# Moving the lo subtraction of two weight pieces per round from VectorE to GpSimd in a float32 decoder trunk

## The chip, the cores and the metric

The kernel runs on one NeuronCore of a Trainium2 chip. The metric is the time of one execution on the device in microseconds (us), as the runtime measures it for the core. A few runs of each kernel are timed and the median is quoted; one more execution is taken with the hardware profiler, and its rows are what is read below.

## What is computed

Two decoder layers on 256 tokens of width 2048, in float32. Each layer mixes tokens (differential attention in the first, dilated attention in the second), attends to 256 memory tokens, and ends in an MLP. The change lies in the MLP alone:

```
hm = _rmsnorm(x, g_mlp[i])
x = x + jnp.square(jax.nn.relu(hm @ w_mlp1[i])) @ w_mlp2[i]
```

with `w_mlp1` 2048 x 8192 and `w_mlp2` 8192 x 2048.

## The kernel before

**Precision.** TensorE multiplies in the format fp32r, which keeps fewer bits than float32. So every operand is held as a pair: `hi` is the value rounded to fp32r, made by ScalarE, and `lo` is value minus `hi`. A product is three passes, hi by hi, hi by lo and lo by hi (`passes`, L609 to L612, one matmul each: L610, L611, L612).

**Units and rounds.** The 8192 hidden columns are cut into eight units of 1024. Unit 0 is computed plainly; units 1 to 7 with a scheme of seven block products per step, eight steps (`step_up`) per unit. While a unit is being made, the unit before it is multiplied with `w_mlp2`. One such round c has eight groups g; group g runs one step of a later unit (on PSUM tiles `p1` to `p7`) and then one `group_down` (24 matmuls into `psd`) for a block n = g // 2 of 512 output columns and a token half t = g % 2. For each n the round needs four weight pieces k = 0, 2, 4, 6, sixteen per round, each a tile of 128 x 1024 which serves the matmuls k and k + 1 of `group_down`.

**A piece.** `piece_hi` (L693) loads the piece into `raw_d` by a DMA that SyncE (SP) issues, and ScalarE (ACT) makes `hi_d` (L699). `piece_lo` (L702) makes `lo_d` by a subtraction on VectorE (DVE, L705). The buffer of `raw_d` comes free for a later load when `lo_d` has been made. The pieces with k = 6 use the ring of buffers "ux", which also holds `b` and `o`, the weights of the steps.

**The weights of a step.** `up_weights` (L210) loads `b` and `o` and makes sums and pairs from them: `s` (DVE, L229), `bh` (ACT) and `bl` (DVE), `o` (L233 and L235), `oh`, `sh` and `sl`, `th` and `tl`. On DVE all of these read two tiles in SBUF.

**The passage.** The square of the ReLU of a unit is finished as four blocks `u`. `to_hT` turns them: TensorE transposes a block (four transposes, L688) into the PSUM tile `pu`, ACT writes the hi part of `hT` (L117), DVE the lo part (L118, one input in PSUM and one in SBUF). The four blocks are turned one at a time, two of them inside the step of group 0 and two inside that of group 1, and a PSUM bank is needed for each. This is the passage from one unit to the next: group 0 of rounds 1 to 6, so six in a layer and twelve in the program. At a passage the pieces of n = 0 are made as follows: k = 0 and the hi of k = 2 at the end of the round before, the lo of k = 2 at the start of group 0, k = 4 and k = 6 after its step.

**What sets the order.** This part runs under `tc.manual_schedule()`: every engine executes its instructions in the order in which the code issues them, and semaphores make one engine wait for another. GpSimd (POOL) issues only the DMAs of `add_down` here (L725), which add a finished `part` (made by ACT at L724 from `psd`) to `x_sb`.

Of the kernel before, what the change touches and what calls it, by code (L numbers as in the profile page):

```python
# [9 lines left out]
F32 = mybir.dt.float32  # L10
# [4 lines left out]
ALU = mybir.AluOpType  # L15
# [43 lines left out]
def trunk(ctx: ExitStack, tc: tile.TileContext, x, mem, g_attn, w_in, w_out, lambda_qk,  # L59
          subln_g, g_mem, w_mem_kv, g_mlp, w_mlp1, w_mlp2, g_final, out):  # L60
    nc = tc.nc
# [17 lines left out]
    def load_weights(src, k, c, nm, other=False):  # L79

        if other:
            raw = upool.tile([P, 1024], F32, tag="ux", bufs=UX, name=f"raw_{nm}")
        else:
            raw = wpool.tile([P, 1024], F32, tag="raw", bufs=RAW, name=f"raw_{nm}")
        nc.sync.dma_start(raw.rearrange("p (k c) -> p k c", c=c), src.rearrange("(k p) c -> p k c", p=P))
        return raw
# [355 lines left out]
    for i in range(DEPTH):  # L442
# [194 lines left out]
        def prep_up(c, kp):  # L637

            making = up_weights(w_mlp1[i], kp, c * 1024, f"{i}{c}{kp}")
            for _ in range(3):  # L640
                next(making)
                yield
            facts[c, kp] = next(making)

        def step_up(c, kp, between=None):


            if kp == 0:
                banks[c] = {n: bank([P, 512], f"{n}_{i}{c}", n in ("p1", "p2", "p5", "p7")) for n in facts[c, 0]}
            order = ("p1", "p2", "p6", "p3", "p7", "p5", "p4") if kp == 0 else ("p1", "p3", "p2", "p5", "p7", "p6", "p4")  # L650
            made = facts.pop((c, kp))
            for j, n in enumerate(order):
                if between and j in between:
                    between[j]()
                hi, lo = made[n]
                passes(banks[c][n], comb[kp][:, FACTORS.index(n)], hi, lo, kp == 0, kp == KP - 1)

        def end_up(c):


            nm, ps = f"{i}{c}", banks.pop(c)
            c1, u2, u3, u4 = (work.tile([P, 512], F32, tag="tmp", bufs=TMP, name=f"t{n}_{nm}") for n in range(4))
            nc.scalar.activation(c1, ps["p1"], AF.Copy)
            yield
            c11, m12, c21, m22 = (work.tile([P, 512], F32, tag="ev", bufs=EV, name=f"u{n}_{nm}") for n in range(4))
            nc.vector.tensor_tensor(c11, c1, ps["p2"], op=ALU.add)
            nc.vector.tensor_tensor(u2, c1, ps["p6"], op=ALU.subtract)
            squared(c11, c11, 1.0)
            nc.vector.tensor_tensor(u4, u2, ps["p5"], op=ALU.add)
            nc.vector.tensor_tensor(m12, u4, ps["p3"], op=ALU.add)  # L670
            squared(m12, m12, -1.0)
            nc.vector.tensor_tensor(u3, u2, ps["p7"], op=ALU.add)
            nc.vector.tensor_tensor(m22, u3, ps["p5"], op=ALU.add)
            nc.vector.tensor_tensor(c21, u3, ps["p4"], op=ALU.add)
            ublk[c] = ((c11, 0, 0), (m12, 0, 1), (c21, 1, 0), (m22, 1, 1))
            yield
            squared(c21, c21, 1.0)
            yield
            squared(m22, m22, -1.0)

        def to_hT(c):

            for f in range(2):
                hT[c, f] = act_tile(f"hT{i}{c}{f}")
            for n, (u, t, f) in enumerate(ublk[c]):
                pt = bank([P, 4, P], f"pu_{i}{c}{n}")
                for k in range(4):
                    nc.tensor.transpose(pt[:, k], u[:, k * P:(k + 1) * P], ident)  # L688
                cols = slice(t * P, (t + 1) * P)
                split(hT[c, f][:, :, 0, cols], hT[c, f][:, :, 1, cols], pt)  # L690
                yield

        def piece_hi(c, n, k):  # L693

            r0 = c * 1024 + k * P
            w, nm = w_mlp2[i][r0:r0 + 256, n * 512:(n + 1) * 512], f"d{i}{c}{n}{k}"
            raw = load_weights(w, 2, 512, nm, k == 6)
            hi = wpool.tile([P, 1024], F32R, tag="whi", bufs=WH, name=f"hi_{nm}")
            nc.scalar.activation(hi, raw, AF.Copy)  # L699
            dw[c, n, k] = raw, hi, nm  # L700

        def piece_lo(c, n, k):  # L702
            raw, hi, nm = dw[c, n, k]
            lo = wpool.tile([P, 1024], F32R, tag="wlo", bufs=WH, name=f"lo_{nm}")
            nc.vector.tensor_tensor(lo, raw, hi.bitcast(F32), op=ALU.subtract)  # L705
            dw[c, n, k], dw[c, n, k + 1] = ((hi[:, a:a + 512], lo[:, a:a + 512]) for a in (0, 512))

        def prep_down(c, n, halves):

            for h in halves:  # L710
                for k in (4 * h, 4 * h + 2):
                    piece_hi(c, n, k)
                    piece_lo(c, n, k)
# [37 lines left out]
        def run(steps):  # L751
            for _ in steps:
                pass
# [3 lines left out]
        with tc.manual_schedule():  # L757
            run(prep_up(1, 0))
            prep_down(0, 0, (0,))
            run(first)  # L760
            turned = to_hT(0)
            prep = prep_up(1, 1)
            step_up(1, 0, {2: lambda: (next(turned), next(prep)), 5: lambda: next(turned)})
            run(prep)
            for c in range(NC - 1):
                for g in range(8):
                    uc, kp = (c + 1, g + 1) if g < 7 else (c + 2, 0)
                    pc, pk = (c + 1, g + 2) if g < 6 else (c + 2, g - 6)
                    prep = prep_up(pc, pk) if pc < NC else iter(())
                    n, t = g // 2, g % 2  # L770
                    more = (c, n + 1) if n < 3 else (c + 1, 0)
                    if g == 0 and c:
                        def turn_first():
                            next(turned)
                            next(ending)
                            next(prep)

                        def turn_second():
                            next(turned)
                            next(prep)  # L780

                        turned = to_hT(c)
                        piece_lo(c, 0, 2)
                        step_up(uc, kp, {2: turn_first, 4: turn_second})
                        prep_down(c, 0, (1,))
                        next(prep)
                        run(ending)
                        run(prep)
                    elif g == 0:
                        step_up(uc, kp)  # L790
                        prep_down(c, 0, (1,))
                        run(prep)
                    elif g == 1:
                        step_up(uc, kp, {2: lambda: (next(turned), next(prep)), 4: lambda: run(turned)})
                        run(prep)
                    elif g == 6:
                        step_up(uc, kp)
                        ending = end_up(c + 1)
                        next(ending)
                        run(prep)  # L800
                        next(ending)
                    elif g == 7 and uc < NC:
                        step_up(uc, kp)
                        run(prep)
                        piece_hi(*more, 0)
                        piece_lo(*more, 0)
                    elif g == 7:
                        run(ending)
                        turned = to_hT(c + 1)
                        next(turned)  # L810
                        next(turned)
                        piece_hi(*more, 0)
                        piece_lo(*more, 0)
                    else:
                        step_up(uc, kp)
                        run(prep)
                    if t == 1 and g < 7:
                        prep_down(*more, (0,))
                        piece_hi(*more, 4)
                    add_down(c, n, t, group_down(c, n, t, False))  # L820
                    if t == 1 and g < 7:
                        piece_hi(*more, 6)
                        piece_lo(*more, 4)
                        piece_lo(*more, 6)
                    elif t == 1:
                        piece_hi(*more, 2)
            run(turned)
            piece_lo(NC - 1, 0, 2)
            prep_down(NC - 1, 0, (1,))
# [71 lines left out]
```

## Time and profile before

| | |
|---|---|
| time, median of 3 runs | 2197.18 us (2194.75 to 2198.06) |
| the profiled execution | 2197.42 us |
| its span, first to last instruction | 2195.6 us |
| TensorE (PE) matmul busy | 2169.9 us, 99% |
| VectorE (DVE) busy | 1711.9 us, 78% |
| ScalarE (ACT) busy | 1327.4 us, 60% |
| GpSimd (POOL) busy | 114.0 us, 5% |
| mean granted TensorE clock | 0.998 of full speed |

How to read it: the profiled execution lies 1.8 us above its span and 0.24 us above the median, so sums made against it hold for the median as well. PEld is the weight load of TensorE, which runs beside its matmuls. Rows of a timeline give start and duration in us from the span's start, and in square brackets how long the engine stood idle before the row and what released it; rows of one form that follow each other are merged into one with a count.

### The profile page before, as it was taken

How to read it: one execution, taken by the hardware profiler on the slowest of the kernel's cores; microseconds unless marked ns; L12 is line 12 of the kernel's file. 1: busy time of each engine (PE TensorE's matmuls, PEld its weight loads, DVE VectorE, ACT ScalarE, POOL GpSimd, SP SyncE). 2: the span in 40 equal slices, each digit the busy share in tenths (PEclk: the TensorE clock that was granted, in tenths of full speed). 3: DMA queues.
4: the chain of work that ended last, by engine and by line, in shares of the span. 5: the costliest groups of instructions: out<-in, count | busy, mean ns of one | idle time of the engine just before them, and what ended most of it. 6: DMA issues, size and time to landing. Idle time of an engine off the chain costs nothing.

```text
span 2195.6 us, 28498 instructions
## 1 busy us (share of the span) xinstructions
PE 2169.9 (99%) x10358; PEld 1791.5 (82%) x10358; DVE 1711.9 (78%) x2084; ACT 1327.4 (60%) x1840; POOL 114.0 (5%) x146
## 2 busy tenths in 40 slices
PE   9999999999999999999999999999999999999998
PEld 7888878887888887888888888888788888888886
DVE  6557766667999998999966655566899999999985
ACT  7445555565667666676655544455566666766764
POOL 0000000000000000000000000000000000000000
PEclk9999999999999999999999999999999999999999
DMA  7655555566787877877656555556777778778674
GB/s 235 199 184 163 164 163 181 167 185 216 224 243 199 238 225 209 248 210 219 200 172 192 155 177 178 182 178 185 236 212 233 219 219 235 205 229 239 200 213 149
DMA packets 262399, 443.50 MB, mean 202 GB/s; under 512 B 14497, under 2 KB 80242, under 8 KB 262002
## 3 DMA queue, kind: packets, MB, share of 16 engines
q1 hardware_dynamic: 245856, 412.14, 60.0%
q0 software_dynamic: 16128, 29.37, 7.5%
q8 instruction: 81, 1.33, 0.2%
q14 instruction: 60, 0.49, 0.1%
q10 hardware_dynamic: 274, 0.17, 0.0%
HBM read 409.12 MB, written 3.15 MB: 188 GB/s over the span
## 4 chain that ended last, share of the span: by engine, by line
PE 94%; ACT 2%; DVE 2%; issue 1%; DMA 1%; SPq 0%; POOL 0%; POOLq 0%; DVEq 0%; ACTq 0%
PE psd L611 10%; PE psd L612 10%; PE psd L610 10%; PE p L610 8%; PE p L611 7%; PE p L612 7%; PE ps_k L145 4%; PE ps_q L145 4%; PE pso L166 3%; PE pso L167 3%; PE pso L165 3%; PE ps_q L141 2%; PE ps_k L141 2%; PE psv L165 2%; PE psv L166 2%; PE psv L167 2%
## 5 line engine op out<-in xcount | busy, mean ns | idle before, releaser
L611 PE MATMUL psd<-lo_d,hT 128*128 128x512 f32 x1008 | 392.0, 390 | 0.6 <-DVE lo_d L705 0.6
L612 PE MATMUL psd<-hi_d,hT 128*128 128x512 f32 x1008 | 391.8, 389 | 0.0
L610 PE MATMUL psd<-hi_d,hT 128*128 128x512 f32 x1008 | 391.0, 390 | 0.0
L705 DVE TENSOR_TENSOR lo_d<-raw_d,hi_d 128x1024 fp32r<-128x1024 f32 x252 | 297.4, 1219 | 47.8 <-ACT hi_d L699 47.5
L699 ACT ACTIVATE hi_d<-raw_d 128x1024 fp32r<-128x1024 f32 x252 | 260.2, 1052 | 35.1 <-PE psd L612 13.9
L117 ACT ACTIVATE th<-o 128x1024 fp32r<-128x1024 f32 x112 | 119.0, 1063 | 183.6 <-DVE o L235 157.4
L611 PEld LDWEIGHTS psd<-lo_d,hT 128*128 128x128 f32 x1008 | 189.2, 188 | 40.5 <-DVE lo_d L705 1.5
L612 PEld LDWEIGHTS psd<-hi_d,hT 128*128 128x128 f32 x1008 | 189.2, 188 | 39.9 <-DVE hT L118 0.8
L610 PEld LDWEIGHTS psd<-hi_d,hT 128*128 128x128 f32 x1008 | 189.2, 188 | 39.3
L118 DVE TENSOR_TENSOR bl<-b,bh 128x1024 fp32r<-128x1024 f32 x112 | 136.8, 1221 | 39.0 <-ACT bh L117 39.0
L725 POOL DMA_DIRECT2D x_sb<-part x112 | 96.6, 863 | 1182.1 <-ACT part L724 1176.6
L117 ACT ACTIVATE sh<-s 128x1024 fp32r<-128x1024 f32 x112 | 118.5, 1058 | 54.3 <-DVE s L229 41.7
L118 DVE TENSOR_TENSOR tl<-o,th 128x1024 fp32r<-128x1024 f32 x112 | 137.2, 1225 | 6.2 <-ACT th L117 0.3
L229 DVE TENSOR_TENSOR s<-b,o 128x1024 f32<-128x1024 f32 x112 | 136.3, 1217 | 5.5 <-DMA o<-in_w_mlp_dram 5.5
L118 DVE TENSOR_TENSOR sl<-s,sh 128x1024 fp32r<-128x1024 f32 x112 | 136.4, 1218 | 0.0
L117 ACT ACTIVATE bh<-b 128x1024 fp32r<-128x1024 f32 x112 | 118.1, 1054 | 13.1 <-PE p L611 12.4
L145 PE MATMUL ps_k<-xT,hi_k 128*128 128x512 f32 x384 | 122.3, 398 | 0.0
L145 PE MATMUL ps_q<-xT,hi_q 128*128 128x512 f32 x384 | 122.0, 399 | 0.0
L724 ACT ACTIVATE part<-psd,rsq 128x512 f32<-128x512 f32 x112 | 76.4, 683 | 57.2 <-PE psd L612 56.5
L118 DVE TENSOR_TENSOR lo_v<-raw_v,hi_v 128x1024 fp32r<-128x1024 f32 x48 | 58.8, 1224 | 50.2 <-ACT hi_v L117 50.1
L610 PE MATMUL p<-sh,cb_xm 128*128 128x512 f32 x224 | 89.8, 401 | 0.0
L610 PE MATMUL p<-bh,cb_xm 128*128 128x512 f32 x224 | 88.7, 396 | 0.8 <-ACT bh L117 0.5
(331 smaller groups left out, 4880.0 us busy)
## 6 DMA issues: line engine op xcount, KB each, us to landing
raw_d<-in_w_mlp_dram SPq DMA_DIRECT2D x252, 512.0 KB, 6.1
b<-in_w_mlp_dram SPq DMA_DIRECT2D x112, 512.0 KB, 4.0
o<-in_w_mlp_dram SPq DMA_DIRECT2D x112, 512.0 KB, 3.8
x_sb<-part POOLq DMA_DIRECT2D x112, 256.0 KB, 5.9
raw_q<-in_w_in_dram SPq DMA_DIRECT2D x48, 512.0 KB, 3.6
raw_k<-in_w_in_dram SPq DMA_DIRECT2D x48, 512.0 KB, 4.0
raw_v<-in_w_in_dram SPq DMA_DIRECT2D x48, 512.0 KB, 3.7
raw_o<-in_w_out_dram SPq DMA_DIRECT2D x48, 512.0 KB, 3.7
```

The lines of the kernel that those rows point to most:

```text
L117: nc.scalar.activation(dst_hi, src, AF.Copy)
L118: nc.vector.tensor_tensor(dst_lo, src, dst_hi.bitcast(F32), op=ALU.subtract)
L145: nc.tensor.matmul(ps[j].rearrange("p h t -> p (h t)"), hi[:, j * P:(j + 1) * P], a.rearrange("p h t -> p (h t)"), **f)
L165: nc.tensor.matmul(ps[t], ah, hi, start=first and kk == 0, stop=False)
L166: nc.tensor.matmul(ps[t], ah, lo, start=False, stop=False)
L167: nc.tensor.matmul(ps[t], al, hi, start=False, stop=last and kk == 3)
L229: nc.vector.tensor_tensor(s, b, o[:, 0:1].to_broadcast([P, 2, 512]), op=ALU.add)
L610: nc.tensor.matmul(ps, acts[:, 0, :], hi, start=first, stop=False)
L611: nc.tensor.matmul(ps, acts[:, 0, :], lo, start=False, stop=False)
L612: nc.tensor.matmul(ps, acts[:, 1, :], hi, start=False, stop=last)
L699: nc.scalar.activation(hi, raw, AF.Copy)
L705: nc.vector.tensor_tensor(lo, raw, hi.bitcast(F32), op=ALU.subtract)
```

## The change

`piece_lo` takes the engine as an argument. At a passage (g = 0, c > 0) the subtraction for k = 2 and that for k = 6 of n = 0 are issued on GpSimd; that for k = 4 stays on VectorE, and so do all others. That is two of sixteen pieces in rounds 1 to 6 of each layer, 24 instructions in all.

```diff
-        def piece_lo(c, n, k):
+        def piece_lo(c, n, k, eng=nc.vector):
             raw, hi, nm = dw[c, n, k]
             lo = wpool.tile([P, 1024], F32R, tag="wlo", bufs=WH, name=f"lo_{nm}")
-            nc.vector.tensor_tensor(lo, raw, hi.bitcast(F32), op=ALU.subtract)
+            eng.tensor_tensor(lo, raw, hi.bitcast(F32), op=ALU.subtract)
...
                         turned = to_hT(c)
-                        piece_lo(c, 0, 2)
+                        piece_lo(c, 0, 2, nc.gpsimd)
                         step_up(uc, kp, {2: turn_first, 4: turn_second})
-                        prep_down(c, 0, (1,))
+                        for k in (4, 6):
+                            piece_hi(c, 0, k)
+                            piece_lo(c, 0, k, nc.gpsimd if k == 6 else nc.vector)
                         next(prep)
                         run(ending)
                         run(prep)
```

The first place is VectorE at the first passage of layer 0. The digits behind `lo_d` are layer, round, n and k; behind `s_`, `bl_` and `o_` they are layer, unit and step; `hT010` and `hT011` are the two column halves of unit 1. Before:

```order
L705 TENSOR_TENSOR lo_d0100_5330<-raw_d0100_5326,hi_d0100_5328 128x1024
L705 TENSOR_TENSOR lo_d0102_5364<-raw_d0102_5360,hi_d0102_5362 128x1024
L118 TENSOR_TENSOR hT010_5372<-pu_010_5374,hT010_5372 128x4x128
L229 TENSOR_TENSOR s_022_5387<-b_022_5383,o_022_5385 128x1024
L118 TENSOR_TENSOR hT011_5373<-pu_011_5396,hT011_5373 128x4x128
L118 TENSOR_TENSOR bl_022_5404<-b_022_5383,bh_022_5403 128x1024
L705 TENSOR_TENSOR lo_d0104_5420<-raw_d0104_5416,hi_d0104_5418 128x1024
L705 TENSOR_TENSOR lo_d0106_5426<-raw_d0106_5422,hi_d0106_5424 128x1024
L233 TENSOR_TENSOR o_022_5385<-s_022_5387,b_022_5383 128x512
```

The two subtractions `lo_d0102` and `lo_d0106` are what goes. With the change the same place on VectorE reads:

```order
L705 TENSOR_TENSOR lo_d0100_5330<-raw_d0100_5326,hi_d0100_5328 128x1024
L118 TENSOR_TENSOR hT010_5372<-pu_010_5374,hT010_5372 128x4x128
L229 TENSOR_TENSOR s_022_5387<-b_022_5383,o_022_5385 128x1024
L118 TENSOR_TENSOR hT011_5373<-pu_011_5396,hT011_5373 128x4x128
L118 TENSOR_TENSOR bl_022_5404<-b_022_5383,bh_022_5403 128x1024
L705 TENSOR_TENSOR lo_d0104_5420<-raw_d0104_5416,hi_d0104_5418 128x1024
L233 TENSOR_TENSOR o_022_5385<-s_022_5387,b_022_5383 128x512
```

The first `hT` follows `lo_d0100` directly, and `o` follows `lo_d0104`; nothing else changes places. The second place is GpSimd between the last DMA of round 0 and the first of round 1:

```order
@@ -30,4 +30,6 @@
 L725 DMA x_sb_76<-part0030_5272 128x512
 L725 DMA x_sb_76<-part0031_5357 128x512
+L705 TENSOR_TENSOR lo_d0102_5364<-raw_d0102_5360,hi_d0102_5362 128x1024
+L705 TENSOR_TENSOR lo_d0106_5426<-raw_d0106_5422,hi_d0106_5424 128x1024
 L725 DMA x_sb_76<-part0100_5467 128x512
 L725 DMA x_sb_76<-part0101_5569 128x512
```

Both subtractions stand behind the DMA of `part0031` and ahead of that of `part0100`. The order on TensorE, ScalarE and SyncE is the same as before.

## Rows read from the trace of the kernel before

**Rows 1.** The page: busy time of TensorE; the chain that ended last, by engine.

```profile
PE 2169.9 (99%) x10358; PEld 1791.5 (82%) x10358; DVE 1711.9 (78%) x2084; ACT 1327.4 (60%) x1840; POOL 114.0 (5%) x146
...
PE 94%; ACT 2%; DVE 2%; issue 1%; DMA 1%; SPq 0%; POOL 0%; POOLq 0%; DVEq 0%; ACTq 0%
```

**Rows 2.** Waits of TensorE over the span: us in total, times, longest.

```profile
PE pu L688 <- DVE hT L118: 4.7, 12, 0.4
```

**Rows 3.** Timeline of DVE at the first passage: start, us, instruction [idle before].

```profile
603.99 1.22 DVE L705 TENSOR_TENSOR lo_d<-raw_d,hi_d 128x1024 fp32r<-128x1024 f32 x1 [0.58 <-ACT hi_d L699]
605.13 0.68 DVE L118 TENSOR_TENSOR hT<-pu,hT 128x512 fp32r<-128x512 f32 x1
605.73 1.22 DVE L229 TENSOR_TENSOR s<-b,o 128x1024 f32<-128x1024 f32 x1
607.19 0.69 DVE L118 TENSOR_TENSOR hT<-pu,hT 128x512 fp32r<-128x512 f32 x1 [0.25 <-ACT hT L117]
608.13 1.23 DVE L118 TENSOR_TENSOR bl<-b,bh 128x1024 fp32r<-128x1024 f32 x1 [0.25 <-ACT bh L117]
609.28 2.35 DVE L705 TENSOR_TENSOR lo_d<-raw_d,hi_d 128x1024 fp32r<-128x1024 f32 x2
611.55 0.69 DVE L233 TENSOR_TENSOR o<-s,b 128x512 f32<-128x512 f32 x1
...
614.75 1.22 DVE L118 TENSOR_TENSOR tl<-o,th 128x1024 fp32r<-128x1024 f32 x1
```

**Rows 4.** Timeline of ACT at the same passage.

```profile
604.12 0.60 ACT L117 ACTIVATE hT<-pu 128x512 fp32r<-128x512 f32 x1 [0.16 <-PE pu L688]
...
608.00 2.00 ACT L699 ACTIVATE hi_d<-raw_d 128x1024 fp32r<-128x1024 f32 x2
...
613.65 1.06 ACT L117 ACTIVATE th<-o 128x1024 fp32r<-128x1024 f32 x1 [1.01 <-DVE o L235]
614.62 0.67 ACT L724 ACTIVATE part<-psd,rsq 128x512 f32<-128x512 f32 x1
```

**Rows 5.** Timeline of PE at the same passage: the second four transposes.

```profile
605.87 0.66 PE L688 MATMUL pu<-ident,u 128*128 128x128 f32 x4 [0.40 <-DVE hT L118]
```

**Rows 6.** Timeline of PEld there: lo of pieces k = 4 and k = 6, next transposes.

```profile
611.16 0.19 PEld L611 LDWEIGHTS psd<-lo_d,hT 128*128 128x128 f32 x1
...
612.52 0.19 PEld L611 LDWEIGHTS psd<-lo_d,hT 128*128 128x128 f32 x1
...
615.34 0.42 PEld L688 LDWEIGHTS pu<-ident,u 128*128 128x128 f32 x4 [0.37 <-ACT part L724]
```

**Rows 7.** Timeline of POOL at the same passage: its only instruction.

```profile
603.42 0.87 POOL L725 DMA_DIRECT2D x_sb<-part  x1 [6.57 <-ACT part L724]
```

**Rows 8.** Timeline of POOL at the start of layer 1: instructions that read SBUF.

```profile
1160.07 1.45 POOL L350 TENSOR_SCALAR_AFFINE_SELECT dist<-dist 128x256 f32<-128x256 f32 x1
...
1162.31 0.28 POOL L348 TENSOR_SCALAR_AFFINE_SELECT dist<-dist 128x128 f32<-128x128 f32 x1
1162.56 0.39 POOL L350 TENSOR_SCALAR_AFFINE_SELECT dist<-dist 128x256 f32<-128x256 f32 x1
```

**Rows 9.** Timeline of DVE at the same time.

```profile
1160.05 1.21 DVE L118 TENSOR_TENSOR lo_qm<-raw_qm,hi_qm 128x1024 fp32r<-128x1024 f32 x1
...
1162.02 0.86 DVE L186 SCALAR_TENSOR_TENSOR xT<-pt_xa,gT,xT 128x256 fp32r<-128x256 f32 x2
```

**Rows 10.** Groups of POOL: a two-input instruction of one column (busy us, mean ns).

```profile
L871 POOL TENSOR_TENSOR rf<-base,nhalf 128x1 f32<-128x1 f32 x2 | 1.3, 646 | 45.6 <-DVE base L862 43.0 <-DVE base L868 2.6
```

**Rows 11.** Timelines of POOL and of DVE in layer 0, after a token mixer.

```profile
345.94 1.01 POOL L248 TENSOR_TENSOR ro<-v,nhalf 128x4 f32<-128x4 f32 x1 [306.81 <-DVE v L247]
...
346.36 1.23 DVE L118 TENSOR_TENSOR lo_v<-raw_v,hi_v 128x1024 fp32r<-128x1024 f32 x1 [0.50 <-ACT hi_v L117]
```

**Rows 12.** SP's queue: a load behind the passage; DVE: the first reader of its data.

```profile
612.26 0.37 SPq L224 DMA_DIRECT2D b<-in_w_mlp_dram  x1
...
629.72 1.22 DVE L229 TENSOR_TENSOR s<-b,o 128x1024 f32<-128x1024 f32 x1
```

## Prediction, made before the changed kernel was run

> **What bounds the kernel now.** I read the page first. TensorE is busy for 99% of the span and the chain that ended last is 94% TensorE [rows 1], so only what makes TensorE wait, or stops a wait, can change the time. The list of TensorE's waits comes next: the largest wait of all is "pu <- DVE hT", 4.7 us in 12 times, 0.40 us each [rows 2]. Twelve is the number of passages. The timelines of a passage then show where it comes from. VectorE stands idle for 0.58 us until ScalarE has made `hi_d` of piece 2, subtracts from 603.99, and only at 605.13 begins the lo of `hT` [rows 3], which it could have begun when ScalarE's part was done, at 604.12 + 0.60 = 604.72 [rows 4]. The second transposes wait for that until 605.87, 0.40 us of it as idle time of TensorE [rows 5].
>
> **What is removed.** With the subtraction for k = 2 gone, VectorE starts `hT` at about 604.75 in place of 605.13. The gain is 0.38 us per passage, all of it inside the 0.40 us that TensorE stands idle; every date of TensorE and ScalarE behind it moves 0.38 up. Twelve times 0.38 is 4.6 us, if nothing is given back.
>
> **What is added: how long one subtraction takes on GpSimd.** The trace of before has none of this shape; call it D. GpSimd's select takes 0.28 us for 128 columns and 0.39 us for 256 [rows 8], so 0.11 us per 128 columns, 0.88 us for 1024, and 0.17 us fixed. Lower bound: both inputs at the pace of one, 0.17 + 0.88 = 1.05 us. Upper bound: a two-input instruction of a single column takes 0.65 us [rows 10], all of that fixed, and two inputs and the output follow one another: 0.65 + 3 x 0.88 = 3.3 us. I take the two inputs one after the other, 1.76 us, and a fixed part between 0.17 and 0.65, 0.4 us: D = 2.2 us, since the two-input row is the nearest in kind and the select the nearest in size. The Trainium skill, "GPSIMD Engine Reference", section "Performance versus the Vector engine", gives 4497 ns for a float32 add of 2048 columns; half of that, 2.25 us, would make the sum below 1.2 us larger, an estimate from that page which no run here shows yet.
>
> **What is added: two engines on one read path.** At 1160.07 a select of 256 columns, which waits for no semaphore, took 1.45 us in place of 0.39 [rows 8]. Beside it VectorE ran a subtraction with two SBUF inputs from 1160.05 to 1161.26, at its usual 1.21 us [rows 9]. The later selects ran at their fastest beside a VectorE instruction with one input in PSUM at 1162.02 [rows 8, 9]. So GpSimd stood still until the two-input instruction of VectorE was through, and an input in PSUM does not do that. The Trainium skill, "SBUF — State Buffer", section "Who interferes with whom", states this for both directions: of a VectorE instruction with two SBUF inputs and a GpSimd one that reads SBUF, the first to start keeps the other out until it ends. The trace agrees for the direction above; against it, VectorE started a two-input subtraction at 346.36 inside a GpSimd instruction of 1.01 us and took its usual 1.23 us [rows 11]. That GpSimd instruction reads only four columns, so it may have done its reading. By that rule the sum is the one that follows; without it the sum is the first rival. I take exclusion in both directions, because the one collision of long reads in the trace was total.
>
> **The sum of a passage, with D = 2.2.** GpSimd's DMA ends at 603.42 + 0.87 = 604.3 [rows 7]; the lo of k = 2 runs from 604.3 to 604.3 + D = 606.5. VectorE's `hT` (PSUM) is not touched, but `s`, with two SBUF inputs, could start at 605.35 and now starts at 606.5 (605.73 before). The spacing of VectorE's instructions is 1.14 us for 1024 columns and 0.60 us for `hT` [rows 3]. So `hT` 607.64, `bl` 608.24, lo of k = 4 from 609.38 to 610.6, in general 608.4 + D. TensorE wants that at 611.16 - 0.38 = 610.78 [rows 6]: in time by 0.2 us.
>
> The hi of k = 6 is ready at 610.0 - 0.38 = 609.62 [rows 4]. VectorE is 0.24 us into the lo of k = 4 then, so GpSimd begins at 610.6 and ends at 608.4 + 2D = 612.8. TensorE wants it at 612.52 - 0.38 = 612.14 [rows 6]: a wait of 0.66 us, the one that I expect in place of the removed one.
>
> VectorE meanwhile may not start `o`, which reads `s` and `b` in SBUF, before 612.8 (611.55 before, so 1.25 us late in spite of one instruction less). Behind `o` wait ScalarE's `th` and behind that `part`: from `o` at 611.55 to the end of `part` at 615.29 it is 3.74 us, with `th` idle for VectorE ahead of it [rows 3, 4]. The transposes of group 1 already wait for `part` [rows 6]. They move by the same 1.25 us, more than the -0.38 + 0.66 = +0.28 us by which TensorE comes there anyway; so `part` sets the end. Net per passage: 608.4 + 2D - 611.55 = 2D - 3.15 = **+1.25 us**. Twelve passages give 15.0 us. Against the profiled execution, 2197.42 us, that is 2212.4; the median of before is 0.24 us lower, so I predict **2212 us**.
>
> At nothing I cost: the loads that wait for GpSimd in place of VectorE. The load of `b` at 612.26 waited for the lo of k = 6 and would be about a microsecond later; its data are first read at 629.72 [rows 12], which leaves over 15 us. GpSimd's next DMA needs `part` at 615 and finds the engine free. Less work on VectorE is worth nothing in itself, as TensorE never waited for its load as a whole.
>
> **Rivals.**
>
> *No exclusion that matters, the time falls.* If VectorE and GpSimd share the path, lo of k = 6 runs 609.62 to 611.82, ahead of 612.14, and `o` starts earlier than before. The gain of 12 x 0.38 = 4.6 us stands: 2193 us. For it speaks the undisturbed subtraction at 346.36 [rows 11], against it the stretched select [rows 8]. It decides only if D is below 2.5, since 609.62 + D must stay under 612.14. Chance 0.17.
>
> *GpSimd takes the path first at the second piece.* The lo of k = 4 starts at 607.18 + D. Above D = 2.44 that is later than 609.62: GpSimd goes first, lo of k = 4 ends at 610.84 + D, TensorE waits D + 0.06 for it, net D - 0.32 = 2.1 to 3.0 us per passage. Twelve times: 2223 to 2233 us. Chance 0.17.
>
> *VectorE always goes first.* Then `s` and `o` are on time, but GpSimd gets in for k = 6 only when the run of two-input instructions is through with `tl`, which ends at 614.75 + 1.22 before [rows 3], about 1.5 us earlier with one instruction less and the 0.38. Done at 614.4 + 2.2 = 616.6, a wait of 4.5 us, net 4.1 us, 2246 us. After the select at 1160.07 [rows 8] got in as soon as one instruction of VectorE ended, I hold this for unlikely: 0.08.
>
> *D is so short that exclusion costs nothing.* With 2D - 3.15 between -0.38 and +0.35, so D from 1.4 to 1.75, the time lies between 2193 and 2201.6 us. It needs two inputs read at nearly the pace of one. Chance 0.08.
>
> That the change does not do what it says is ruled out by the order of the instructions: both subtractions stand on GpSimd at every one of the twelve passages.
>
> **How the numbers follow.** The forecast, exclusion with D from 1.75 to 2.44, has the chance 0.5; its own range is 2201.6 to 2218 us. The range for 8 in 10 takes in the two cases at 2193 to 2202 and the lower part of the case from 2223 on: 2192 to 2226 us. What a measurement of this kernel can tell from no change is about 0.2%, 4.4 us: 2192.8 to 2201.6. The first rival lies at that edge, so half of it and a little of the short D count as faster, 0.12; the rest of both as the same, 0.14; all else is slower, 0.74.
>
> **What would show it.** In the changed kernel's timelines: the wait "pu <- DVE hT" falls from 0.40 us to next to nothing in the 12 passages; the two subtractions on GpSimd take about 2.2 us where they are not held, and the second starts or stretches with the end of VectorE's lo of k = 4; VectorE's `s` and `o` take longer than their 1.22 and 0.69 us or start late; TensorE waits about 0.7 us for `lo_d` from GpSimd; the transposes of group 1 wait about 1.3 us for `part`. The forecast is wrong if VectorE's `s` and `o` keep their durations beside GpSimd, or if D lies outside 1.75 to 2.44 us.

## The result, and the profile after

| | before | changed |
|---|---|---|
| median of the runs, us | 2197.07 (2194.75 to 2198.06, 6 runs) | 2210.48 (2209.53 to 2211.59, 6 runs) |
| profiled execution, us | 2197.42 | 2211.22 |
| its span, us | 2195.6 | 2209.4 |

The change made the kernel **slower**: 1.0065 times the time of before, with a 95% interval from 1.0054 to 1.0076. The medians are 13.4 us apart, the spans of the two profiled executions 13.8 us. The forecast was 2212 us.

The page of the changed kernel, busy time by engine and the chain that ended last:

```profile
PE 2177.6 (99%) x10358; PEld 1790.9 (81%) x10358; DVE 1723.9 (78%) x2060; ACT 1327.2 (60%) x1840; POOL 180.9 (8%) x170
...
PE 91%; DVE 6%; ACT 2%; issue 1%; DMA 0%; SPq 0%; POOL 0%; POOLq 0%; DVEq 0%; ACTq 0%
```

Against [rows 1], two things are odd. VectorE has 24 instructions fewer (2060 in place of 2084) and is busy *longer*, by 12.0 us, and its share of the chain went from 2% to 6%. At 1.22 us each, the 24 subtractions that left it were 29.3 us of work; so some 41 us of busy time came in without an instruction. That is the first sign of what happened.

The list of TensorE's waits, after:

```profile
PE pu L688 <- ACT part L724: 9.7, 12, 0.8
PE psd L610 <- DVE hT L118: 2.6, 12, 0.3
```

The wait "pu <- DVE hT" of [rows 2] is gone, as meant. Two others took its place, 12 times each: the transposes of group 1 wait for `part`, and the first matmul of `psd` waits for the second `hT`.

The timeline of PE at the first passage gives the price of one. After:

```profile
602.55 0.60 PE L688 MATMUL pu<-ident,u 128*128 128x128 f32 x4
...
604.57 0.66 PE L688 MATMUL pu<-ident,u 128*128 128x128 f32 x4
...
607.54 0.50 PE L610 MATMUL psd<-hi_d,hT 128*128 128x512 f32 x1 [0.23 <-DVE hT L118]
...
612.06 0.50 PE L611 MATMUL psd<-lo_d,hT 128*128 128x512 f32 x1
...
615.67 0.66 PE L688 MATMUL pu<-ident,u 128*128 128x128 f32 x4 [0.82 <-ACT part L724]
...
617.74 0.66 PE L688 MATMUL pu<-ident,u 128*128 128x128 f32 x4
```

And of the kernel before, the first and the last two of the same four transposes (the second stands in [rows 5]):

```profile
603.48 0.60 PE L688 MATMUL pu<-ident,u 128*128 128x128 f32 x4
...
615.35 0.66 PE L688 MATMUL pu<-ident,u 128*128 128x128 f32 x4
...
617.41 0.66 PE L688 MATMUL pu<-ident,u 128*128 128x128 f32 x4
```

From the first transposes of a passage to the second ones of group 1 is the **ruler** that I use below. It is 617.41 - 603.48 = 13.93 us before and 617.74 - 602.55 = 15.19 us after: +1.26 us, and 12 times that is 15.1 us. The whole passage lies 0.93 us earlier in the profile of after, though nothing in front of it was changed; over all the profiles of this study the first transposes start anywhere from 601.08 to 603.48. So such a sum meets a difference of whole times to some 2 us, and dates of the two kernels are compared here after adding 0.93 us to those of after.

The timeline of POOL of the changed kernel. The first three rows are the first passage, the last is the second one:

```profile
602.49 0.87 POOL L725 DMA_DIRECT2D x_sb<-part  x1 [6.56 <-DVE lo_d L705]
603.11 2.68 POOL L705 TENSOR_TENSOR lo_d<-raw_d,hi_d 128x1024 fp32r<-128x1024 f32 x1
608.78 3.23 POOL L705 TENSOR_TENSOR lo_d<-raw_d,hi_d 128x1024 fp32r<-128x1024 f32 x1 [2.99 <-ACT hi_d L699]
...
689.60 2.39 POOL L705 TENSOR_TENSOR lo_d<-raw_d,hi_d 128x1024 fp32r<-128x1024 f32 x1 [0.18 <-issue]
```

The timeline of DVE at the first passage, with the same columns:

```profile
603.82 0.69 DVE L118 TENSOR_TENSOR hT<-pu,hT 128x512 fp32r<-128x512 f32 x1 [1.34 <-ACT hT L117]
604.43 2.46 DVE L229 TENSOR_TENSOR s<-b,o 128x1024 f32<-128x1024 f32 x1
606.81 0.68 DVE L118 TENSOR_TENSOR hT<-pu,hT 128x512 fp32r<-128x512 f32 x1
607.41 1.21 DVE L118 TENSOR_TENSOR bl<-b,bh 128x1024 fp32r<-128x1024 f32 x1
608.54 1.21 DVE L705 TENSOR_TENSOR lo_d<-raw_d,hi_d 128x1024 fp32r<-128x1024 f32 x1
609.67 2.88 DVE L233 TENSOR_TENSOR o<-s,b 128x512 f32<-128x512 f32 x1
612.48 0.68 DVE L118 TENSOR_TENSOR oh<-o,oh 128x512 fp32r<-128x512 f32 x1
```

Read the second column against [rows 3]. `s` takes 2.46 us in place of 1.22, and `o` 2.88 in place of 0.69. Neither has an idle time in brackets: a held instruction is no wait in this trace, it is a *longer* instruction. No semaphore is behind it either: in the trace of the changed kernel neither `s` nor `o` waits, at any of the twelve passages, for the one that GpSimd's subtraction sets. And the first `hT`, with one input in PSUM, lies wholly inside GpSimd's subtraction and keeps its 0.69 us. `s` is held while GpSimd makes the lo of k = 2 (until 605.79), `o` while it makes that of k = 6 (until 612.01). Twelve times 1.24 + 2.19 us is the 41 us of busy time without an instruction. GpSimd in its turn is held at the second piece: its subtraction is issued at 608.78, inside VectorE's lo of k = 4 (608.54 to 609.75), and takes 3.23 us, where the one at 689.60 took 2.39.

What stands behind `o`, in the timeline of ACT (compare [rows 4], where `th` had waited 1.01 us):

```profile
613.98 1.06 ACT L117 ACTIVATE th<-o 128x1024 fp32r<-128x1024 f32 x1 [2.63 <-DVE o L235]
614.94 0.67 ACT L724 ACTIVATE part<-psd,rsq 128x512 f32<-128x512 f32 x1
```

And in the timeline of PEld, which answers to [rows 6]: the wait for the second `hT`, that for GpSimd's lo of k = 6, and that for `part`:

```profile
607.54 0.19 PEld L610 LDWEIGHTS psd<-hi_d,hT 128*128 128x128 f32 x1 [0.67 <-DVE hT L118]
...
612.06 0.19 PEld L611 LDWEIGHTS psd<-lo_d,hT 128*128 128x128 f32 x1 [0.35 <-POOL lo_d L705]
...
615.66 0.42 PEld L688 LDWEIGHTS pu<-ident,u 128*128 128x128 f32 x4 [1.24 <-ACT part L724]
```

### The profile page after: what moved, and what is told of

It reads as the page before. It is cut to its first block, busy times and chain, and to the rows that moved or that the text cites. A ratio compares the mean times of both kernels' runs of the same rounds, so it can differ in the third digit from the quotient of the medians.

```text
span 2209.4 us, 28545 instructions
## 1 busy us (share of the span) xinstructions
PE 2177.6 (99%) x10358; PEld 1790.9 (81%) x10358; DVE 1723.9 (78%) x2060; ACT 1327.2 (60%) x1840; POOL 180.9 (8%) x170
## 4 chain that ended last, share of the span: by engine, by line
PE 91%; DVE 6%; ACT 2%; issue 1%; DMA 0%; SPq 0%; POOL 0%; POOLq 0%; DVEq 0%; ACTq 0%
PE psd L611 9%; PE psd L612 9%; PE psd L610 9%; PE p L610 7%; PE p L611 7%; PE p L612 7%; PE ps_k L145 4%; PE ps_q L145 4%; PE pso L166 3%; PE pso L167 3%; PE pso L165 3%; PE ps_q L141 2%; PE ps_k L141 2%; PE psv L165 2%; PE psv L167 2%; PE psv L166 2%
## 5 line engine op out<-in xcount | busy, mean ns | idle before, releaser
L705 DVE TENSOR_TENSOR lo_d<-raw_d,hi_d 128x1024 fp32r<-128x1024 f32 x228 | 269.1, 1220 | 41.0 <-ACT hi_d L699 40.7
L229 DVE TENSOR_TENSOR s<-b,o 128x1024 f32<-128x1024 f32 x112 | 151.1, 1349 | 5.8 <-DMA o<-in_w_mlp_dram 5.8
L233 DVE TENSOR_TENSOR o<-s,b 128x512 f32<-128x512 f32 x112 | 103.2, 922 | 0.0
```

The costliest lines, as they stand in the source:

```text
L229: nc.vector.tensor_tensor(s, b, o[:, 0:1].to_broadcast([P, 2, 512]), op=ALU.add)
L705: eng.tensor_tensor(lo, raw, hi.bitcast(F32), op=ALU.subtract)
```

## The experiments

The theory: VectorE's instructions with two SBUF inputs and GpSimd's subtraction keep each other out, whichever is in first, and of the two that VectorE loses time on, `s` and `o`, the one that counts is `o`, by way of `th` and `part`. The rivals: GpSimd's subtraction is merely slow, and TensorE waits for its result; GpSimd's *writing*, or its being active at all, is what slows VectorE; ScalarE's order is to blame, not the shared path. The kernel before ran beside the first four at 2195.70 us (median of 16 runs) and beside the last three at 2196.95 us (of 25).

### Only the piece k = 2 on GpSimd

```diff
-    piece_lo(c, 0, k, nc.gpsimd if k == 6 else nc.vector)
+    piece_lo(c, 0, k, nc.vector)
```

> Only the lo of k = 2 goes to GpSimd; that for k = 6 is back on VectorE. Theory (exclusion, and the loss lies in VectorE's o being held by the lo of k = 6): s is still held by about 1.2 us, but VectorE has one subtraction less in front of o, so o is late by only about 0.2 us and the transposes of group 1 with it: 12 x 0.2 = 2 us, 2199 us (2197 to 2201). Rival one (the loss comes from the hold of s, through the second hT and the first psd matmul): 2205 us or more. Rival two (no exclusion at all): the 0.38 us stand, 2192.5 us.

Measured: 2198.42 us (2196.70 to 2199.88, 11 runs), 1.0011 times before, interval 1.0002 to 1.0020. The timeline of DVE at the first passage:

```profile
604.20 2.45 DVE L229 TENSOR_TENSOR s<-b,o 128x1024 f32<-128x1024 f32 x1
...
610.58 0.68 DVE L233 TENSOR_TENSOR o<-s,b 128x512 f32<-128x512 f32 x1
```

`s` is held as in the full change, `o` not at all. The timeline of PE gives a ruler of 616.44 - 602.32 = 14.12 us, +0.19:

```profile
602.32 0.60 PE L688 MATMUL pu<-ident,u 128*128 128x128 f32 x4
...
616.44 0.66 PE L688 MATMUL pu<-ident,u 128*128 128x128 f32 x4
```

Counted from the first transposes, `o` starts at 610.58 - 602.32 = 8.26 us, before at 611.55 - 603.48 = 8.07: 0.19 us late too. `s` starts 0.37 us earlier than before (604.20 - 602.32 against 605.73 - 603.48 [rows 3]); its hold, 2.45 - 1.22 = 1.23 us, uses that up, and with it the two idle times that VectorE had behind `s` [rows 3]; the rest is the delay. Each of those shows as 0.25 us, but is worth about 0.33 between starts (1.46 us from `s` to the second `hT`, where instructions that follow without a wait start 1.14 apart, as their records overlap): 1.23 - 0.37 - 0.66 = 0.20. So the piece of k = 2 by itself removes TensorE's wait of 0.40 us and still gains nothing.

### Only the piece k = 6 on GpSimd

```diff
-    piece_lo(c, 0, 2, nc.gpsimd)
+    piece_lo(c, 0, 2)
```

> Only the lo of k = 6 goes to GpSimd; that for k = 2 is back on VectorE. Theory: the wait of the second transposes for hT is back at 0.40 us, GpSimd is let in when VectorE's lo of k = 4 ends and holds o until about 1.05 us after its time of before; the transposes of group 1 move by the same, 12 x 1.05 = 12.6 us, 2209.7 us (2207 to 2212). Rival one (the hold of s costs the time): about 2197 to 2200 us.

Measured: 2208.38 us (2207.96 to 2210.12, 5 runs), 1.0061 times before, interval 1.0047 to 1.0074. DVE's timeline, then TensorE's waits:

```profile
603.61 1.22 DVE L229 TENSOR_TENSOR s<-b,o 128x1024 f32<-128x1024 f32 x1
...
608.30 2.89 DVE L233 TENSOR_TENSOR o<-s,b 128x512 f32<-128x512 f32 x1
```

```profile
PE pu L688 <- ACT part L724: 9.5, 12, 0.8
PE pu L688 <- DVE hT L118: 4.8, 12, 0.4
```

Now `s` is free and `o` held; the wait for `hT` is back and that for `part` is there in full. Nearly all of the loss of the change is this one piece.

### `part` ahead of `th` on ScalarE

In the branch of group 0, `run(prep)`, which issues `th` and `tl` of the next step's weights, goes behind the step that makes `part`; `o` stays where it was:

```diff
     run(ending)
-    run(prep)
...
     add_down(c, n, t, group_down(c, n, t, False))
+    if g == 0 and c:
+        run(prep)
```

> Both subtractions on GpSimd as in the change; at a passage the last stage of the step's weights (th on ScalarE, tl on VectorE) is issued behind part, so that part no longer waits for o. Theory (o, th, part, then the transposes is the path that sets the loss): o is held as before, but the transposes of group 1 come when TensorE is there, about 0.9 us earlier than in the changed kernel; the next transposes wait for an hT that now stands behind tl, which gives back about a third: 12 x 0.55 = 6.5 us less than the changed kernel, 2204 us (2201 to 2207). Rival (TensorE's wait for lo_d from GpSimd is what the change costs): no better than 2209 us.

Measured: 2203.11 us (2201.12 to 2203.77, 5 runs), 1.0032 times before, interval 1.0020 to 1.0045: about half of the loss. The timeline of DVE:

```profile
609.05 2.89 DVE L233 TENSOR_TENSOR o<-s,b 128x512 f32<-128x512 f32 x1
...
615.72 0.68 DVE L118 TENSOR_TENSOR hT<-pu,hT 128x512 fp32r<-128x512 f32 x1
```

and that of PE:

```profile
614.08 0.60 PE L688 MATMUL pu<-ident,u 128*128 128x128 f32 x4
...
616.46 0.66 PE L688 MATMUL pu<-ident,u 128*128 128x128 f32 x4 [0.41 <-DVE hT L118]
```

`o` is held as long as ever (2.89 us), but nothing waits for `part` any more. The ruler is 616.46 - 601.93 = 14.53 us, +0.60. Of that, 0.28 us is there at the first transposes of group 1 already (614.08 - 601.93 = 12.15 us, before 615.35 - 603.48 = 11.87): TensorE comes there later by its own waits, for the second `hT`, which stands behind the held `s`, and for GpSimd's lo of k = 6, less what the second transposes gained. The other 0.32 us comes out one step further on: VectorE's own run of instructions behind `o` is late (and `tl` now waits 0.17 us for the later `th`), `hT` of group 1 starts at 615.72, and the second transposes wait 0.41 us for it. So ScalarE's order carries half of the loss to TensorE. What is left comes from the hold of `s`, TensorE's wait for GpSimd, and the hold of `o`; no run parts these three.

### GpSimd writes, and reads nothing

```diff
-    eng.tensor_tensor(lo, raw, hi.bitcast(F32), op=ALU.subtract)
+    if eng is nc.gpsimd:
+        for _ in range(2):
+            eng.memset(raw, 0.0)
+        lo = hi
...
```

> Leaves out the two subtractions of a passage (the hi part stands in for the lo part of k = 2 and k = 6): GpSimd fills the loaded tile twice with a constant in their place, about 1.9 us of work that writes SBUF and reads nothing, starting when hi is made. TensorE does not wait for it. Theory (VectorE is held only by GpSimd instructions that read): s keeps 1.22 us and o 0.69 us, the gain of 0.38 us at hT stands and part no longer waits for o: 2192 us (2190.5 to 2193.5). Rival (any work of GpSimd in SBUF holds VectorE): s and o are stretched by 0.6 to 1.2 us and the time is 2203 us or more.

Measured: 2189.24 us (2188.51 to 2190.87, 6 runs), 0.9970 times before, interval 0.9959 to 0.9982. POOL's timeline, then DVE's:

```profile
603.63 2.26 POOL L706 MEMSET raw_d<- 128x1024 f32 x2
...
609.30 1.97 POOL L706 MEMSET raw_d<- 128x1024 f32 x2 [3.41 <-ACT hi_d L699]
```

```profile
604.97 1.21 DVE L229 TENSOR_TENSOR s<-b,o 128x1024 f32<-128x1024 f32 x1
...
609.66 0.68 DVE L233 TENSOR_TENSOR o<-s,b 128x512 f32<-128x512 f32 x1
```

GpSimd is at work at the same two places nearly as long (two fills of about 1.0 us each for one subtraction), `s` runs beside the first pair and `o` inside the second, and both have the durations of [rows 3]. It is neither GpSimd's activity nor its writing that holds VectorE. The time is 2.8 us lower than the likeliest that I had expected and below its range, since with no hold `o` runs earlier than in the kernel before and `part` with it: the ruler is 616.50 - 603.10 = 13.40 us, -0.53, of which 0.37 is the wait for `hT`.

### Without GpSimd: `s` in VectorE's idle time

Against the kernel *before*: VectorE idles 0.58 us for `hi_d` of k = 2 [rows 3]. Here `s`, whose inputs are there, goes into that place, and the lo of k = 2 behind the first `hT`.

```diff
 def turn_first():
     next(turned)
     next(ending)
-    next(prep)
+    piece_lo(c, 0, 2)
...
-    piece_lo(c, 0, 2)
+    next(prep)
     step_up(uc, kp, {2: turn_first, 4: turn_second})
```

> GpSimd makes no piece. At a passage VectorE makes s ahead of the first hT, in the 1.3 us in which it would stand idle, and the lo of k = 2 behind the first hT. Theory (the gain of the change lies in the order on VectorE alone, and was to be had without GpSimd): the first hT 0.38 us earlier, lo of k = 2 in time for TensorE, o about 0.4 us earlier than before, so the transposes of group 1 move up by 0.4 to 0.5 us: 12 x 0.42 = 5 us less than the kernel before, 2191 us (2190 to 2193). Rival (VectorE's load at the passage is what binds, whatever its order): no change, 2195.7 us.

Measured: **2191.59 us** (2190.60 to 2192.46, 11 runs), 0.9977 times before, interval 0.9968 to 0.9986: faster than both kernels. The timeline of DVE:

```profile
602.30 1.22 DVE L229 TENSOR_TENSOR s<-b,o 128x1024 f32<-128x1024 f32 x1
603.75 0.69 DVE L118 TENSOR_TENSOR hT<-pu,hT 128x512 fp32r<-128x512 f32 x1 [0.23 <-ACT hT L117]
604.36 1.21 DVE L705 TENSOR_TENSOR lo_d<-raw_d,hi_d 128x1024 fp32r<-128x1024 f32 x1
...
610.19 0.68 DVE L233 TENSOR_TENSOR o<-s,b 128x512 f32<-128x512 f32 x1
```

The first `hT` now waits for ScalarE alone, and the same work stands in another order. The ruler is 616.06 - 602.49 = 13.57 us, -0.36: nearly the whole of the 0.38 us that the change had meant to gain.

### The piece k = 2 on GpSimd, with `s` early

Against the changed kernel: `next(prep)`, which issues `s`, stands ahead of `piece_lo(c, 0, 2, nc.gpsimd)`, no longer in `turn_first`, and the piece of k = 6 is VectorE's.

```diff
 def turn_first():
     next(turned)
     next(ending)
-    next(prep)
...
+    next(prep)
     piece_lo(c, 0, 2, nc.gpsimd)
...
-    piece_lo(c, 0, k, nc.gpsimd if k == 6 else nc.vector)
+    piece_lo(c, 0, k, nc.vector)
```

> The lo of k = 2 on GpSimd as in the run with k = 2 alone, but VectorE makes s ahead of it, so that VectorE has nothing with two SBUF inputs to do while GpSimd reads. Theory (the hold of s and nothing else gave back the gain of 0.38 us there): s, bl and o at their usual durations, GpSimd's subtraction held to the end of s and then 2.3 to 2.4 us; 0.4 to 0.5 us less per passage than before, 2190.5 us (2189.5 to 2192.5). Rival (something else of work on GpSimd costs the time, such as its DMA or its semaphore): about 2198 us as in that run.

Measured: 2190.97 us (2190.03 to 2193.40, 11 runs), 0.9976 times before, interval 0.9967 to 0.9984. It is not to be told from the version without GpSimd (2191.59 us, overlapping intervals). DVE's timeline and POOL's:

```profile
602.68 1.22 DVE L229 TENSOR_TENSOR s<-b,o 128x1024 f32<-128x1024 f32 x1
```

```profile
603.39 2.76 POOL L705 TENSOR_TENSOR lo_d<-raw_d,hi_d 128x1024 fp32r<-128x1024 f32 x1
```

With `s` out of the way, GpSimd's subtraction, once it has started to read, stands beside nothing that reads two inputs from SBUF, and costs nothing, slow as it is. It is held itself at its start: `s` ends at 603.90, and from there to 606.15 it is 2.25 us. The ruler is 616.41 - 602.84 = 13.57 us, the same to the hundredth as without GpSimd.

### GpSimd reads one input

```diff
-    eng.tensor_tensor(lo, raw, hi.bitcast(F32), op=ALU.subtract)
+    if eng is nc.gpsimd:
+        eng.tensor_copy(lo, raw)
...
```

> Leaves out the subtraction in the 24 pieces: GpSimd copies the loaded tile into the lo tile, one SBUF input, estimated at about 1.0 us from the slope of the selects. Theory (any GpSimd instruction that reads SBUF keeps VectorE's two-input instructions out while it reads): the copy of k = 6 is held to the end of VectorE's lo of k = 4, and o is stretched from 0.69 to about 1.7 us; the time is near that of the kernel before, 2194 us (2191 to 2198), since o then begins when it did before. Rival (only a GpSimd instruction with two inputs shuts VectorE out): o keeps 0.69 us, 2190 us.

Measured: 2190.81 us (2189.59 to 2192.57, 8 runs), 0.9975 times before, interval 0.9965 to 0.9986. A miss, by the fault of the experiment. The timelines of POOL and of DVE:

```profile
601.58 2.34 POOL L706 CAST lo_d<-raw_d 128x1024 fp32r<-128x1024 f32 x2
```

```profile
602.96 2.05 DVE L229 TENSOR_TENSOR s<-b,o 128x1024 f32<-128x1024 f32 x1
...
607.80 0.68 DVE L233 TENSOR_TENSOR o<-s,b 128x512 f32<-128x512 f32 x1
```

A copy reads `raw` and not `hi_d`, so that of k = 6 no longer waits for ScalarE: both ran at the start, were through 3.9 us ahead of `o`, and `o` was never met. As a time it decides nothing. One thing it does show, against the rival above: `s` took 2.05 us in place of 1.22 beside a copy that reads a single input, so a GpSimd instruction need not read two inputs to hold a two-input VectorE instruction.

### All of them by one ruler

| version | ruler, us | against before | x 12 | medians apart, us |
|---|---|---|---|---|
| the change | 15.19 | +1.26 | +15.1 | +13.4 |
| only k = 2 | 14.12 | +0.19 | +2.3 | +2.7 |
| only k = 6 | 15.01 | +1.08 | +13.0 | +12.7 |
| `part` ahead of `th` | 14.53 | +0.60 | +7.2 | +7.4 |
| GpSimd only writes | 13.40 | -0.53 | -6.4 | -6.5 |
| `s` early, no GpSimd | 13.57 | -0.36 | -4.3 | -5.4 |
| `s` early, k = 2 on GpSimd | 13.57 | -0.36 | -4.3 | -6.0 |
| GpSimd reads one input | 13.54 | -0.39 | -4.7 | -6.1 |

The ruler of the first passage, twelve times, gives every one of the eight differences to within 2 us, the scatter named above. In each version the other eleven passages lie within 0.11 us of the first. Outside the passages the profiles differ from that of before by 0.4 to 2.4 us ahead of the first passage, where the kernels are alike, and by under 0.4 us in all the rest.

Of the rivals, that of GpSimd's writing or mere activity falls by the write-only version. That of a merely slow GpSimd falls at k = 2 by the version with `s` early, in which the subtraction is as slow and costs nothing; at k = 6 TensorE does wait for it, but only 0.35 us on PEld and not at all on PE's own list. ScalarE's order is no cause of its own: it is how half of the loss reaches TensorE.

## Why the prediction was right

**What was removed.** The second transposes come at 604.57 + 0.93 = 605.50, 0.37 us earlier than at 605.87 [rows 5]; 0.38 had been worked out, and "pu <- DVE hT" left the list. Right.

**D, the time of one subtraction.** Not held, it is 2.39 us by the row at 689.60 (the only one of the twelve pieces k = 2 whose record does not begin inside a DMA's; the others show 2.58 to 2.68), and 2.25 us from the end of `s` in the version with `s` early. I had taken 2.2 and bounds of 1.05 to 3.3. The row of the two-input instruction [rows 10] and the select [rows 8] together were a fair guide; the term is 0.05 to 0.2 us small. The Trainium skill, "GPSIMD Engine Reference", section "Performance versus the Vector engine", had led to an estimate of 2.25 us, at the lower of the two measured values. A larger D would have brought the rival in which GpSimd takes the second piece first, from 2.44 us on: 2.39 is 0.05 us short of that. D thus lies in the upper part of the 1.75 to 2.44 us that the forecast allowed, and well above the 1.4 to 1.75 of the rival with a short D.

**Exclusion both ways.** This was the step on which the sign hung, and it held in both directions: `s` +1.24 and `o` +2.19 us on VectorE, the second subtraction +0.84 us on GpSimd (3.23 against 2.39). The single-piece versions show each hold where its piece is and nowhere else, and the write-only version shows neither. The Trainium skill, "SBUF — State Buffer", section "Who interferes with whom", has VectorE with two SBUF inputs contend with a GpSimd instruction that reads SBUF and not with one that only writes it; this case's rows agree on both counts (2.46 and 2.88 us beside the subtraction, 1.21 and 0.68 us beside the fills). The row that spoke against it, VectorE's subtraction at 346.36, which was not held though it started 0.59 us before the end of a GpSimd instruction on four columns [rows 11], was not taken apart; that GpSimd had done its reading stays a guess.

**The dates of the passage**, predicted and measured (after + 0.93):

| | predicted | measured |
|---|---|---|
| second `hT` on VectorE starts | 607.64 | 607.74 |
| lo of k = 4 starts | 609.38 | 609.47 |
| lo of k = 6 on GpSimd ends | 612.8 | 612.94 |
| `oh`, behind `o`, against before | +1.25 | +1.26 |
| transposes of group 1 start | 615.34 + 1.25 = 616.59 | 616.60 |

VectorE was in first at the second piece, as taken, by 608.54 against 608.78, in all twelve passages. So the rivals did not come: that without exclusion falls by the two holds, that in which VectorE always goes first by `o`, which was kept waiting, and that with GpSimd first by these dates, although narrowly. No version was run in which GpSimd reaches the second piece first; what that would cost stays as worked out.

**The sum.** +1.25 us per passage was +1.26 by the ruler of the first passage. That it met so closely is in part luck. GpSimd's lo of k = 6 ended 0.14 us later than worked out (612.94 against 612.8), since D is larger; but `o` was let in 0.15 us ahead of that end: it ended at 612.55, and 0.69 us before that is 611.86, where GpSimd's row runs to 612.01. The two errors cancel. The twelve rulers (15.14 to 15.29 us, before 13.93 to 13.94) add up to +14.8 us; the spans of the two profiled executions are 13.8 us apart, mostly because the first passage starts 0.93 us earlier in that of after, and the medians 13.4.

**Small things.** The chances of "the same" and "slower" are each 0.01 off what the rivals add up to (0.13 and 0.75), which changes nothing. The load of `b`, costed at nothing, went out 1.7 us later (613.04 + 0.93 against 612.26 [rows 12]), and no wait for it came into the list of TensorE's waits.

**Two details that were wrong** without harm to the sum. I expected TensorE to wait 0.66 us for GpSimd's lo of k = 6; PEld shows 0.35, and the list of PE's own waits does not have it. And I overlooked a wait: the first matmul of `psd` waits for the second `hT` (0.23 us on PE, 0.67 on PEld), because VectorE copies that `hT` out of PSUM only when the held `s` is through. By the code, `psd` takes its bank from the same ring as the transposes `pu`, with three of the four banks held by the `p` tiles of the unit in the making; so it can't start before the transposes are copied out. That is argued from the code, no run took it apart; but on PE the wait appears in the three versions in which GpSimd's subtraction holds `s`, and on PEld also, shorter, in the one in which a copy does (12 times 0.23 us); where `s` is not held it is in neither list. It came ahead of the wait for `lo_d`, and so shortened that one; since `part` sets the end, neither changed the sum. For `part` about 1.3 us had been expected, and PEld shows 1.24.

**What the list of waits leaves out.** TensorE's new idle time is 9.7 + 2.6 - 4.7 = 7.6 us, half of the loss; its busy time rose by 7.7 us [rows 1] for the same matmuls. The records of matmuls overlap: they are 0.39 us long and start 0.23 us apart, so the first 0.16 us of a wait lies inside the record ahead and counts as busy, and the first matmul behind a wait shows 0.50 us (at 607.54 and 612.06). The ruler, from one date to another, does not have that fault.

## What to carry to other kernels

In this kernel, moving an elementwise operation to GpSimd would have freed VectorE only if what stands beside it there read no two inputs from SBUF, as in the version with `s` early. `s` and `o` do, and were held (2.46 and 2.88 us in place of 1.22 and 0.69) until GpSimd was through, which takes 2.39 us for what VectorE does in 1.22. Look for that in durations of instructions (against the same line elsewhere), not in the list of waits, and then follow what waits behind the instruction that would be held: here `o`, `th`, `part` and TensorE. Where an engine idles for one input, first ask whether another of its instructions is ready: two lines in another order gave the whole gain, 0.23%, that the second engine was brought in for.

## What the runs showed of the hardware that was not expected, or only assumed

- `o`, held behind GpSimd's subtraction, went ahead 0.15 us before the end of GpSimd's row (611.86 against 612.01), and `s` 0.12 us before (606.89 - 1.22 = 605.67 against 605.79): the hold is a little shorter than the record.
- When VectorE's lo of k = 4 ended, `o`, the next on VectorE, needed the same path, and GpSimd, which had been waiting since 608.78, got it: VectorE's next instruction did not go ahead of the engine that was waiting. I had assumed this from a single select [rows 8]; it was so in all twelve passages.
- On GpSimd, for 128 x 1024 floats, two fills take 1.97 us, two copies of one input 2.34 us (the first begins inside a DMA's record), and one subtraction of two inputs 2.39 us: about as much as two passes over one input. VectorE's subtraction of that size takes 1.22 us.
- The subtraction's record can begin inside that of the DMA issue ahead of it: at 603.11, while the DMA's ran until 603.36, and it then shows 2.68 us in place of 2.39. So here a duration on GpSimd just behind a DMA issue is too long by 0.2 to 0.3 us.
